# Layer normalisation without affine parameters: separate rings for x and y, tiles of 8 rows, and bn_stats parts combined by GpSimd

## The chip, the cores and the metric

The kernel runs on one core of one Trainium2 chip. The metric is the device time of one execution in microseconds. Each comparison runs both kernels in alternating rounds on the same chip. All runs used here are fast, with the granted clock at 1.0. The profile's span is about 2 us shorter than the time. The changed kernel was timed in one batch and the experiments in three others; the kernel before ran in every batch, and its medians there agree within 0.1 us.

## The reference

```python
def setup_inputs():
    batch, seq, dim = 32, 512, 1024
    return {"x": np.random.randn(batch, seq, dim).astype(np.float32), "eps": 1e-5}

def reference(x, eps):
    mean = np.mean(x, axis=-1, keepdims=True)
    var = np.var(x, axis=-1, keepdims=True)
    return ((x - mean) / np.sqrt(var + eps)).astype(np.float32)
```

There are 16384 rows of 1024 floats: 67.11 MB are read and 67.11 MB are written. With 128 partitions each partition handles 128 rows; "a tile of K rows" below means K rows per partition, and each row is 4 KB there.

## The kernel before

A tile has 4 rows per partition. Loads go out on the SyncE queue and stores on the ScalarE queue; there are six buffers for x and six for y, 48 rows of 4 KB in each partition. A scheduler orders the instructions.

```python
    K = 4
    xin = ctx.enter_context(tc.tile_pool(name="xin", bufs=6))
    yout = ctx.enter_context(tc.tile_pool(name="yout", bufs=6))
    ...
    for t in range(ntiles):                                   # 32 tiles
        xt = xin.tile([P, K, D], fdt)
        nc.sync.dma_start(out=xt, in_=x2[rows].rearrange("(p k) d -> p k d", p=P))
        for k in range(K):
            for s in range(NSUB):                             # two halves of a row
                nc.vector.bn_stats(...)
            nc.vector.bn_aggr(out=mv[:, k, :], in_=stats[:, k, :, :])
        ...                                                   # -mean, var + eps, reciprocal on VectorE
        nc.scalar.activation(out=rstd, in_=ivar, func=AF.Sqrt, bias=0.0, scale=1.0)
        nc.gpsimd.tensor_mul(out=nmr, in0=negmean, in1=rstd)
        for k in range(K):
            nc.scalar.activation(out=yt[:, k, :], in_=xt[:, k, :], func=AF.Identity,
                                 bias=nmr[:, k : k + 1], scale=rstd[:, k : k + 1])
        nc.scalar.dma_start(out=dst, in_=yt)
```

## Time and profile before

| What | Value |
|---|---|
| time | 321.23 us (321.14 to 321.33) |
| span of the profiled run | 319.0 us |
| DMA, mean over the span | 421 GB/s, digit 9 in 38 of 40 slices |
| VectorE / ScalarE / GpSimd busy | 57% / 48% / 2% |

The prediction below shows the lines behind this table and reads them. One more part of the page, the DMA part, has the number of packets (one record for each piece that one DMA engine moves) and, per queue, the packets, the bytes and the time of the packets as a share of 16 engines:

```profile
DMA packets 9222, 134.27 MB, mean 421 GB/s; under 512 B 1024, under 2 KB 1024, under 8 KB 1024
...
q1 hardware_dynamic: 4608, 67.11, 49.6%
q10 hardware_dynamic: 4608, 67.11, 49.2%
```

Each queue has 4096 data packets, 67.11 MB / 4096 = 16 KB, which is the 4 rows of a tile in one partition, and 512 small ones, 16 for each of its 32 transfers. Queue q1 carries the loads and q10 the stores.

### The profile page before, as it was taken

Reading aid. Unit: us, or ns where it says so; the run is one execution under the profiler, and the core shown is the slowest. Engines: PE = TensorE matmul, PEld = TensorE weight load, DVE = VectorE, ACT = ScalarE, POOL = GpSimd, SP = SyncE. Lnnn points to the kernel's source line nnn. Section 1 sums busy time; section 2 is a strip of 40 time slices with the busy share of each in tenths; the row PEclk is TensorE's granted clock in tenths of the full one; section 3 lists DMA queues with packets and bytes.
Section 4 is the critical chain, followed back from the end, with each engine's and each line's share of the span. In section 5 each row is a group of like instructions: output and inputs, shape, how many; then the busy total and the mean of one; then the engine's idle time right before and its main releaser. Section 6 shows DMA issues by size and latency. Waiting matters only on the chain.

```text
span 319.0 us, 926 instructions
## 1 busy us (share of the span) xinstructions
DVE 181.6 (57%) x480; ACT 154.3 (48%) x161; POOL 6.6 (2%) x36
## 2 busy tenths in 40 slices
DVE  0999764457754477544676355765446744467610
ACT  1147491651907419074380833809247091470970
POOL 0000000000000000000000000000000000000000
DMA  7999999999999999999999999999999999999995
GB/s 294 427 405 422 438 431 431 431 429 431 426 429 432 435 431 431 429 427 431 431 433 435 430 431 427 427 431 427 435 438 430 428 431 427 431 427 427 421 427 220
DMA packets 9222, 134.27 MB, mean 421 GB/s; under 512 B 1024, under 2 KB 1024, under 8 KB 1024
## 3 DMA queue, kind: packets, MB, share of 16 engines
q1 hardware_dynamic: 4608, 67.11, 49.6%
q10 hardware_dynamic: 4608, 67.11, 49.2%
q14 instruction: 6, 0.05, 0.0%
HBM read 67.11 MB, written 67.11 MB: 421 GB/s over the span
## 4 chain that ended last, share of the span: by engine, by line
DMA 87%; DVE 4%; issue 3%; ACT 2%; SPq 1%; POOLq 0%; POOL 0%; DVEq 0%
DMA xt<-in_x_dram 87%; DVE stats L53 3%; ACT yt L75 1%; SPq L47 1%; DVE mv L57 0%; DVE ivar L65 0%; DVE negmean L59 0%; POOLq L115 0%; ACT rstd L68 0%; POOL nmr L71 0%; DVE vpe L61 0%; DVEq L65 0%; DVEq L59 0%
## 5 line engine op out<-in xcount | busy, mean ns | idle before, releaser
L53 DVE BATCH_NORM_STATS2 stats<-xt 128x6 f32<-128x512 f32 x256 | 159.4, 665 | 115.3 <-DMA xt<-in_x_dram 115.3
L75 ACT ACTIVATE yt<-xt,nmr,rstd 128x1024 f32<-128x1024 f32 x128 | 146.7, 1227 | 4.7 <-POOL nmr L71 4.5
L68 ACT ACTIVATE rstd<-ivar 128x4 f32<-128x4 f32 x32 | 6.6, 205 | 149.6 <-DVE ivar L65 149.0
L57 DVE BATCH_NORM_AGGREGATE mv<-stats 128x2 f32<-128x12 f32 x128 | 25.1, 196 | 1.1
L71 POOL TENSOR_TENSOR nmr<-negmean,rstd 128x4 f32<-128x4 f32 x32 | 6.3, 198 | 297.9 <-ACT rstd L68 297.9
L65 DVE RECIPROCAL ivar<-vpe 128x4 f32<-128x4 f32 x32 | 5.7, 178 | 3.0
L59 DVE TENSOR_SCALAR negmean<-mv 128x4 f32<-128x4 f32 x32 | 5.4, 170 | 3.1
L61 DVE TENSOR_SCALAR vpe<-mv 128x4 f32<-128x4 f32 x32 | 5.2, 162 | 0.0
L68 ACT ACT_TABLE_LOAD x1 | 1.3, 1283 | 0.7 <-PEq L101 0.7
L101 POOL MEMSET const-float32-0.0<- 128x1 f32 x1 | 0.1, 98 | 0.2 <-issue 0.2
L101 POOL MEMSET const-uint8-127<- 128x1 uint8 x1 | 0.1, 102 | 0.0
L101 POOL MEMSET const-bfloat16-1.0<- 128x1 bf16 x1 | 0.1, 101 | 0.0
L101 POOL MEMSET const-float32-1.0<- 128x1 f32 x1 | 0.1, 98 | 0.0
## 6 DMA issues: line engine op xcount, KB each, us to landing
xt<-in_x_dram SPq DMA_DIRECT2D x32, 2048.0 KB, 38.4
out_dram<-yt ACTq DMA_DIRECT2D x32, 2048.0 KB, 15.5
```

The lines of the kernel that those rows point to most:

```text
L47: nc.sync.dma_start(out=xt, in_=x2[rows].rearrange("(p k) d -> p k d", p=P))
L53: nc.vector.bn_stats(out=stats[:, k, s, :], in_=xt[:, k, s * BN_MAX : (s + 1) * BN_MAX],)
L57: nc.vector.bn_aggr(out=mv[:, k, :], in_=stats[:, k, :, :])
L59: nc.vector.tensor_scalar_mul(out=negmean, in0=mv[:, :, 0], scalar1=-1.0)
L61: nc.vector.tensor_scalar(out=vpe, in0=mv[:, :, 1], scalar1=eps_val, scalar2=None, op0=ALU.add)
L65: nc.vector.reciprocal(out=ivar, in_=vpe)
L68: nc.scalar.activation(out=rstd, in_=ivar, func=AF.Sqrt, bias=0.0, scale=1.0)
L71: nc.gpsimd.tensor_mul(out=nmr, in0=negmean, in1=rstd)
L75: nc.scalar.activation(out=yt[:, k, :], in_=xt[:, k, :], func=AF.Identity, bias=nmr[:, k : k + 1], scale=rstd[:, k : k + 1],)
L101: nc = _bacc.Bacc("TRN2", target_bir_lowering=False, num_devices=1)
```

## The change

The intent is to take the aggregation off VectorE, by combining the parts of bn_stats for eight rows at once on GpSimd, and to use larger tiles: fifteen of 8 rows, then 4, 2, 2. The 48 rows of buffer are kept, divided into a ring of 32 for x and one of 16 for y. The order of instructions is the one written, not a scheduler's.

```diff
+TILES = (8, 8, 8, 8, 8, 8, 8, 8, 8, 8, 8, 8, 8, 8, 8, 4, 2, 2)
+XRING = 32
+YRING = 16
+GROUP = 8
...
-    xin = ctx.enter_context(tc.tile_pool(name="xin", bufs=6))
-    yout = ctx.enter_context(tc.tile_pool(name="yout", bufs=6))
+    xr = rings.tile([P, XRING, D], fdt)
+    yr = rings.tile([P, YRING, D], fdt)
...
-            nc.vector.bn_aggr(out=mv[:, k, :], in_=stats[:, k, :, :])
+        pool_sum(nmean[:, :G], mean4)             # two GpSimd adds
+        nc.gpsimd.tensor_scalar(... scalar1=-1.0 / H, op0=ALU.mult)
+        nc.gpsimd.tensor_tensor(out=dev[:, :G], in0=mean4, in1=<nmean broadcast>, op=ALU.add)
+        nc.gpsimd.tensor_mul(out=dev[:, :G], in0=dev[:, :G], in1=dev[:, :G])
+        nc.gpsimd.tensor_scalar(... scalar1=float(D // H), op0=ALU.mult)
+        nc.gpsimd.tensor_tensor(out=dev[:, :G], in0=dev[:, :G], in1=m2, op=ALU.add)
+        pool_sum(ss[:, :G], dev[:, :G])           # two GpSimd adds
+        nc.scalar.activation(out=std[:, :G], in_=ss[:, :G], func=AF.Sqrt, bias=eps_t, scale=1.0 / D)
+        nc.vector.reciprocal(out=rstd[:, :G], in_=std[:, :G])
...
+    with tc.manual_schedule():
+        for (K, row, xp), (_, _, yp) in zip(place(TILES, XRING), place(TILES, YRING)):
+            nc.sync.dma_start(out=xr[:, xp : xp + K, :], in_=rows_of(x2, row, K))
+            ...
+                group(xr[:, a : a + G, :], yr[:, b : b + G, :], G)
+            nc.scalar.dma_start(out=rows_of(o2, row, K), in_=yr[:, yp : yp + K, :])
```

More of the change, by code (lines that the diff above doesn't have):

```diff
@@ L7, with place @@
 from concourse._compat import with_exitstack
+TILES = (8, 8, 8, 8, 8, 8, 8, 8, 8, 8, 8, 8, 8, 8, 8, 4, 2, 2)
+XRING = 32
+YRING = 16
+GROUP = 8
+def place(tiles, ring):
+    plan, row, pos = [], 0, 0
+    for K in tiles:
+        if pos + K > ring:
+            pos = 0
+        plan.append((K, row, pos))
+        row += K
+        pos += K
+    return plan
 @with_exitstack
@@ L26 @@
     BN_MAX = nc.vector.BN_STATS_FMAX
-    assert D % BN_MAX == 0
     NSUB = D // BN_MAX
-    K = 4
-    rows_per_tile = P * K
-    assert N % rows_per_tile == 0
-    ntiles = N // rows_per_tile
-    xin = ctx.enter_context(tc.tile_pool(name="xin", bufs=6))
-    yout = ctx.enter_context(tc.tile_pool(name="yout", bufs=6))
+    assert sum(TILES) * P == N
+    rings = ctx.enter_context(tc.tile_pool(name="rings", bufs=1))
     st = ctx.enter_context(tc.tile_pool(name="st", bufs=4))
@@ L41, with rows_of, pool_sum, group @@
     ALU = mybir.AluOpType
-    for t in range(ntiles):
-        rows = slice(t * rows_per_tile, (t + 1) * rows_per_tile)
-        xt = xin.tile([P, K, D], fdt)
-        nc.sync.dma_start(out=xt, in_=x2[rows].rearrange("(p k) d -> p k d", p=P))
-        stats = st.tile([P, K, NSUB, 6], fdt)
-        mv = st.tile([P, K, 2], fdt)
-        for k in range(K):
+    xr = rings.tile([P, XRING, D], fdt)
+    yr = rings.tile([P, YRING, D], fdt)
+    eps_t = rings.tile([P, 1], fdt)
+    def rows_of(a, row, K):
+        return a[row * P : (row + K) * P].rearrange("(p k) d -> p k d", p=P)
+    def pool_sum(o, terms):
+        G = terms.shape[1]
+        half = st.tile([P, GROUP, 2], fdt, name="half")
+        nc.gpsimd.tensor_tensor(
+            out=half[:, :G], in0=terms[:, :, 0:2], in1=terms[:, :, 2:4], op=ALU.add
+        )
+        nc.gpsimd.tensor_tensor(
+            out=o, in0=half[:, :G, 0], in1=half[:, :G, 1], op=ALU.add
+        )
+    def group(xs, ys, G):
+        stats = st.tile([P, GROUP, NSUB, 6], fdt, name="stats")
+        for k in range(G):
             for s in range(NSUB):
@@ L54 @@
                     out=stats[:, k, s, :],
-                    in_=xt[:, k, s * BN_MAX : (s + 1) * BN_MAX],
+                    in_=xs[:, k, s * BN_MAX : (s + 1) * BN_MAX],
                 )
-            nc.vector.bn_aggr(out=mv[:, k, :], in_=stats[:, k, :, :])
-        negmean = st.tile([P, K], fdt)
-        nc.vector.tensor_scalar_mul(out=negmean, in0=mv[:, :, 0], scalar1=-1.0)
-        vpe = st.tile([P, K], fdt)
-        nc.vector.tensor_scalar(
-            out=vpe, in0=mv[:, :, 1], scalar1=eps_val, scalar2=None, op0=ALU.add
-        )
@@ L64 @@
-        ivar = st.tile([P, K], fdt)
-        nc.vector.reciprocal(out=ivar, in_=vpe)
-        rstd = st.tile([P, K], fdt)
-        nc.scalar.activation(out=rstd, in_=ivar, func=AF.Sqrt, bias=0.0, scale=1.0)
-        nmr = st.tile([P, K], fdt)
-        nc.gpsimd.tensor_mul(out=nmr, in0=negmean, in1=rstd)
-        yt = yout.tile([P, K, D], fdt)
-        for k in range(K):
+        H = 2 * NSUB
+        parts = stats[:, :G].rearrange("p g s (h c) -> p g (s h) c", h=2)
+        mean4, m2 = parts[:, :, :, 1], parts[:, :, :, 2]
@@ new lines, in group @@
+        nmean = st.tile([P, GROUP], fdt, name="nmean")
+        dev = st.tile([P, GROUP, H], fdt, name="dev")
+        ss = st.tile([P, GROUP], fdt, name="ss")
+        pool_sum(nmean[:, :G], mean4)
+        nc.gpsimd.tensor_scalar(
+            out=nmean[:, :G], in0=nmean[:, :G], scalar1=-1.0 / H, scalar2=None, op0=ALU.mult
+        )
+        nc.gpsimd.tensor_tensor(
+            out=dev[:, :G],
+            in0=mean4,
+            in1=nmean[:, :G].unsqueeze(2).to_broadcast([P, G, H]),
+            op=ALU.add,
+        )
@@ new lines, in group @@
+        nc.gpsimd.tensor_mul(out=dev[:, :G], in0=dev[:, :G], in1=dev[:, :G])
+        nc.gpsimd.tensor_scalar(
+            out=dev[:, :G], in0=dev[:, :G], scalar1=float(D // H), scalar2=None, op0=ALU.mult
+        )
+        nc.gpsimd.tensor_tensor(out=dev[:, :G], in0=dev[:, :G], in1=m2, op=ALU.add)
+        pool_sum(ss[:, :G], dev[:, :G])
+        std = st.tile([P, GROUP], fdt, name="std")
+        nc.scalar.activation(
+            out=std[:, :G], in_=ss[:, :G], func=AF.Sqrt, bias=eps_t, scale=1.0 / D
+        )
@@ L75 @@
+        rstd = st.tile([P, GROUP], fdt, name="rstd")
+        nc.vector.reciprocal(out=rstd[:, :G], in_=std[:, :G])
+        nmr = st.tile([P, GROUP], fdt, name="nmr")
+        nc.gpsimd.tensor_mul(out=nmr[:, :G], in0=nmean[:, :G], in1=rstd[:, :G])
+        for k in range(G):
             nc.scalar.activation(
-                out=yt[:, k, :],
-                in_=xt[:, k, :],
+                out=ys[:, k, :],
+                in_=xs[:, k, :],
                 func=AF.Identity,
@@ L81 @@
             )
-        dst = o2[rows].rearrange("(p k) d -> p k d", p=P)
-        nc.scalar.dma_start(out=dst, in_=yt)
+    with tc.manual_schedule():
+        nc.vector.memset(eps_t, eps_val)
+        for (K, row, xp), (_, _, yp) in zip(place(TILES, XRING), place(TILES, YRING)):
+            nc.sync.dma_start(out=xr[:, xp : xp + K, :], in_=rows_of(x2, row, K))
+            for g in range(0, K, GROUP):
+                G = min(GROUP, K - g)
+                a, b = xp + g, yp + g
+                group(xr[:, a : a + G, :], yr[:, b : b + G, :], G)
+            nc.scalar.dma_start(out=rows_of(o2, row, K), in_=yr[:, yp : yp + K, :])
 _INS = ['x', 'eps']
```

## The prediction

> **What bounds the kernel now.** I read the span slices first, because they say whether one resource is full from end to end.
>
> ```profile
> span 319.0 us, 926 instructions
> ...
> DVE 181.6 (57%) x480; ACT 154.3 (48%) x161; POOL 6.6 (2%) x36
> ...
> DMA  7999999999999999999999999999999999999995
> GB/s 294 427 405 422 438 431 431 431 429 431 426 429 432 435 431 431 429 427 431 431 433 435 430 431 427 427 431 427 435 438 430 428 431 427 431 427 427 421 427 220
> ```
>
> No compute engine is over 57% busy, while the DMA digit is 9 in 38 of 40 slices; only the first and the last slice are not full. Next the chain that ended last and the groups of instructions:
>
> ```profile
> DMA xt<-in_x_dram 87%; DVE stats L53 3%; ACT yt L75 1%; SPq L47 1%; DVE mv L57 0%; DVE ivar L65 0%; DVE negmean L59 0%; POOLq L115 0%; ACT rstd L68 0%; POOL nmr L71 0%; DVE vpe L61 0%; DVEq L65 0%; DVEq L59 0%
> ...
> L53 DVE BATCH_NORM_STATS2 stats<-xt 128x6 f32<-128x512 f32 x256 | 159.4, 665 | 115.3 <-DMA xt<-in_x_dram 115.3
> L75 ACT ACTIVATE yt<-xt,nmr,rstd 128x1024 f32<-128x1024 f32 x128 | 146.7, 1227 | 4.7 <-POOL nmr L71 4.5
> ...
> L57 DVE BATCH_NORM_AGGREGATE mv<-stats 128x2 f32<-128x12 f32 x128 | 25.1, 196 | 1.1
> L71 POOL TENSOR_TENSOR nmr<-negmean,rstd 128x4 f32<-128x4 f32 x32 | 6.3, 198 | 297.9 <-ACT rstd L68 297.9
> ```
>
> VectorE's 115.3 us of idle time before the statistics is all waiting for loads: compute follows the data. Last the stretches (stretch, its length, busy time of DVE, ACT and POOL, clock, DMA share, GB/s):
>
> ```profile
> 0.00:4.00 4.00, 0.00 (x0) 1.28 (x1) 0.20 (x4) 1.00 0.55 143
> 4.00:8.00 4.00, 0.00 (x0) 0.00 (x0) 0.00 (x0) 1.00 1.04 442
> ...
> 20.00:24.00 4.00, 4.00 (x10) 0.21 (x1) 0.20 (x1) 1.00 0.98 373
> ...
> 160.00:200.00 40.00, 22.75 (x60) 19.48 (x21) 0.79 (x4) 1.00 1.01 431
> ...
> 308.00:312.00 4.00, 0.00 (x0) 1.34 (x2) 0.00 (x0) 1.00 0.97 414
> 312.00:316.00 4.00, 0.00 (x0) 0.00 (x0) 0.00 (x0) 1.00 0.80 340
> 316.00:319.00 3.00, 0.00 (x0) 0.00 (x0) 0.00 (x0) 1.00 0.04 16
> ```
>
> The rate is 430 to 432 GB/s in every 40 us stretch from 40 to 280 us, with reads and writes mixed, and much the same with reads alone (442 in 4 to 8 us). The bytes are fixed: 67.11 read and 67.11 written. 134.22 MB / 431 GB/s = 311.4 us. Of the span of 319.0 only 7.6 us are not streaming at 431: the start (4 x (431 - 143) / 431 = 2.7 us), the dip when the first store joins (4 x (431 - 373) / 431 = 0.5 us), the end (312 to 319 us carries 1360 + 48 KB, which is 3.3 us of work, so 3.7 us are lost), and 0.7 us of small dips. A change that leaves the bytes alone can gain from these 7.6 us and nowhere else, unless it raises the 431.
>
> **What the Trainium skill says.** "DMA: Bandwidth & Descriptors", section "Where 436 GB/s comes from", puts the ceiling of a core's DMA ports at 435.2 GB/s. The trace agrees: 431 is 99% of it, so larger transfers can add about 1%, or 3 us, at best. The same passage says that an HBM share of some 358 GB/s binds; the measured 431 contradicts that here, with one core running. "Queues, rings and completion order" of that page says that each DMA engine alternates between its queues packet by packet. The trace agrees: the two queues take 49.6% and 49.2%. "GPSIMD Engine Reference", section 3.1, gives about 2.6 cycles of 1.2 GHz per element for a two-input operation; no instruction of before is long enough to test it (198 ns for 4 elements a partition is nearly all fixed cost).
>
> **The change part by part.** Removed from VectorE: 128 aggregations (25.1 us), and 64 small tensor-scalars (10.6 us); 32 reciprocals become 18. All of that ran beside full DMA, so removing it is worth nothing by itself. Added: per tile nine GpSimd instructions, each waiting for the semaphore of the one before it, as the order of the built program shows. By the row of nmr a 4-element one takes 198 ns; the nine have 8 to 32 elements, at 2.6 cycles / 1.2 GHz = 2.2 ns each beyond four (an estimate from the GPSIMD page): 9 x 198 + 0.32 us = 2.1 us, and with gaps of 0.08 us (in the timeline of before, from the end of rstd to nmr) 2.7 us per tile. The 18 tiles pay about 49 us of GpSimd, in the idle time of an engine that was 2% busy.
>
> The serial chain of one 8-row tile, from the pitches in the timeline of before (0.575 us from one bn_stats to the next, 1.133 us from one row of ACT to the next): 16 bn_stats 15 x 0.575 + 0.67 = 9.3 us, GpSimd 2.7, then Sqrt, reciprocal and nmr at about 0.2 each plus gaps 0.8, ACT 7 x 1.133 + 1.23 = 9.2 us. In the new order VectorE starts tile i+1 only after the reciprocal of tile i, so the statistics cannot repeat faster than 9.3 + 2.7 + 0.8 = 12.8 us. The DMA's own period is 8.39 MB / 431 = 19.5 us, so this is hidden while reads and writes overlap.
>
> The buffers hold 48 rows as before (24 + 24), now 32 for x and 16 for y. **Head.** The first 4.19 MB arrive by 4 + (4194 - 572) / 435 = 12.3 us, with 1.15 us to the wake-up (before: 2097 KB are reached at 7.45, the first bn_stats starts at 8.60), so at 13.45. Statistics end at 22.75, ACT starts at 26.3, the first store is issued at 35.5 us, where before it was at 19.6. But four tiles of loads, 16.8 MB, keep the DMA busy until about 41 us, and load 4 is released at 35.5 as well: no idle DMA. Reads alone and both together run at the same rate, so the late first store only shifts writes to the end. **Middle.** With two y slots, ACT on tile i starts when store i-2 has landed. In 19.5 us it needs 1.2 (landing) + 9.2 + 1.3 (issue to first byte) = 11.7, 7.8 us before the queue would run dry. Loads have about 18 us of slack. **End.** Before the first store flows at 36.6 us, 572 + 435 x 32.6 = 14.8 MB are read. The rest, 52.3 MB at 215.5 GB/s, ends at 279.3 us, and 14.8 MB of writes are left: 0.52 of store 12, stores 13 and 14, and the tiles of 4, 2, 2 rows. Now stores drain at 4.19 MB / 431 = 9.7 us, and a y slot needs 11.7 to come back. Store 12 drains at 284.4; ACT on tile 14 runs 285.7 to 294.9; its bytes flow from 296.1, while store 13 has drained at 294.1: one **gap of 2.0 us**. The small tiles follow without one: tile 15's store is issued at 300.3, 16's about 303.5, 17's about 308.9, and store 14 drains at 305.9, then 310.7, 313.2, 315.6. With the 3.7 us between effective end of bytes and end of span, that is 319.3.
>
> By difference: span 319.0 + 2.0 (gap), less 0.7 for the dips of 401 GB/s around 298 to 306 us and of 310 to 311 us, which the split tail should fill, + 0 for everything that moved on the compute engines = 320.3. The time of before is 2.2 us above its span, so 322.5; the clock sum gives 321.5. I choose 322.0.
>
> **Rivals.**
> (1) The larger transfers raise the rate. For: half as many descriptors of twice the size (32 KB per partition) and fewer transfer boundaries, 36 for 64. Against: 431 of 435 is used already. At 434 GB/s the bytes take 309.3 us, and the time is about 320.
> (2) GpSimd is slower than I take it, and the chain statistics, GpSimd, Sqrt, reciprocal becomes the bound at the end. For: nine dependent steps, a stride of 12 bytes in the reads, nothing of the kind in the profile of before. At 0.6 us each a tile pays 5.4 us: still below 19.5 in the middle, but the last two tiles each wait 2.7 us longer, so the time is some 325.
> (3) Two y slots are too few: a landing that takes several us longer lets the write queue run dry in the middle. Loads then take the free share and finish earlier, and the write-only end grows to as much as five tiles with a 2 us gap each: 329. Against: 7.8 us of slack; stores in before land 8.8 to 20.4 us after their issue, queueing included.
> (4) The freed VectorE makes it faster, as the change intends. Against: VectorE's idle time was 115.3 us and all of it waited for loads. It would make nothing of the time.
>
> **Range and chances.** The floor is start + bytes + end, 2.7 + 309.3 + 3.7 + 2.2 = 317.9 at 434 GB/s; the 2% border is at 314.8, below it, so faster is nearly excluded. Slower needs 327.7, which takes rival 3 or 2 and 3 together. I put 319.3 to 325.5 as the range: rival 1 at its best and rival 2 at its worst are just inside. Chances: faster 0.01, same 0.95, slower 0.04.
>
> **What would show it.** Right: DMA digits of 9 and about 431 GB/s from the second slice to the last but two; VectorE near 9.3 x 16 = 150 us and GpSimd near 50; the first store issued at about 35 us; ACT waiting for stores in the middle; a stretch of lower GB/s near 294 to 296 us. Wrong: middle slices clearly off 431 (rivals 1 and 3), GpSimd steps over 0.4 us, or several dips in the last 40 us.

## The result, and the profile after

The changed kernel took 318.09 us (318.04 to 318.25) against 321.28 us in the same rounds. The ratio is 0.9902, with a 95% interval of 0.9888 to 0.9916. A ratio here is the mean time of one kernel's fast runs over that of the other's of the same rounds, so it is not quite the ratio of the quoted medians. It is 1% faster, inside the 2% that was given a chance of 0.95, but 1.2 us below the stated range of 319.3 to 325.5.

The head of the page of the changed kernel, its DMA part and the first groups of instructions:

```profile
span 316.3 us, 749 instructions
...
DVE 155.6 (49%) x275; ACT 153.4 (49%) x147; POOL 41.5 (13%) x184
...
DMA  8999989999999999999999999999999999999996
...
DMA packets 5189, 134.26 MB, mean 425 GB/s; under 512 B 576, under 2 KB 576, under 8 KB 576
...
q1 hardware_dynamic: 2592, 67.11, 49.7%
q10 hardware_dynamic: 2592, 67.11, 49.2%
...
L113 ACT ACTIVATE yr<-xr,nmr,rstd 128x1024 f32<-128x1024 f32 x128 | 146.7, 1227 | 117.8 <-DMA out_dram<-yr 115.7
L77 DVE BATCH_NORM_STATS2 stats<-xr 128x6 f32<-128x512 f32 x256 | 153.4, 677 | 12.2 <-DMA xr<-in_x_dram 12.2
```

The reader sees that the DMA is still the bound, that VectorE lost 26 us of work and GpSimd gained 35, and that the waiting moved: VectorE hardly waits for loads now, and ScalarE waits 115.7 us for a store to free a y slot. The packets fell from 9222 to 5189, because a tile of 8 rows gives packets of 32 KB.

The stretches of the changed kernel (stretch, its length, busy time of DVE, ACT and POOL, clock, DMA share, GB/s):

```profile
0.00:4.00 4.00, 0.06 (x1) 1.28 (x1) 0.19 (x4) 1.00 0.72 246
4.00:8.00 4.00, 0.00 (x0) 0.00 (x0) 0.00 (x0) 1.00 0.95 410
...
160.00:200.00 40.00, 19.40 (x34) 20.22 (x21) 5.64 (x25) 1.00 1.00 433
...
292.00:296.00 4.00, 2.58 (x5) 0.84 (x3) 0.29 (x2) 1.00 0.95 408
296.00:300.00 4.00, 0.00 (x0) 4.00 (x4) 1.79 (x9) 1.00 1.04 451
...
308.00:312.00 4.00, 0.00 (x0) 1.74 (x2) 0.00 (x0) 1.00 0.97 410
312.00:316.00 4.00, 0.00 (x0) 0.00 (x0) 0.00 (x0) 1.00 0.40 168
```

The span fell by 2.7 us, and the bytes moved per stretch say where. (The view counts a whole packet in the stretch in which it starts. Up to 16 packets of 32 KB, 0.5 MB or 1.2 us of work, are under way at a border, so each of the three terms below can be off by some tenths of a us.) **Middle:** the six stretches from 40 to 280 us have a mean of 432.5 GB/s, where before had 431.0: 240 x 1.5 / 431 = 0.8 us. **Start:** by 280 us the changed kernel has moved 0.69 MB more in all; less the 0.36 MB of the middle, 0.33 MB or some 0.75 us come from the first 40 us. **End:** from 280 us to the end of the span, before moves 14.9 MB in 39.0 us and the changed kernel 14.3 MB in 36.3 us. At 431 GB/s these would take 34.7 and 33.1 us, so 4.3 and 3.2 us are lost: 1.1 us gained. The sum is 2.7 us.

The dip that was forecast near 294 to 296 us is not there: 408 and 451 GB/s. The timeline of ScalarE in the changed kernel shows why the forecast failed. Each of these starts was released by a store that freed a y slot:

```profile
236.35 9.16 ACT L113 ACTIVATE yr<-xr,nmr,rstd 128x1024 f32<-128x1024 f32 x8 [9.41 <-DMA out_dram<-yr]
...
255.74 9.16 ACT L113 ACTIVATE yr<-xr,nmr,rstd 128x1024 f32<-128x1024 f32 x8 [9.49 <-DMA out_dram<-yr]
...
270.83 9.16 ACT L113 ACTIVATE yr<-xr,nmr,rstd 128x1024 f32<-128x1024 f32 x8 [5.21 <-DMA out_dram<-yr]
...
283.35 9.16 ACT L113 ACTIVATE yr<-xr,nmr,rstd 128x1024 f32<-128x1024 f32 x8 [2.65 <-DMA out_dram<-yr]
```

The stores land 19.4 us apart while loads and stores share equally, and then 15.1 and 12.5 us apart, although loads are still in flight. The loads at that time are those of the 4-, 2- and 2-row tiles, with packets of 16 and 8 KB against 32 KB of the stores. If the engines alternate packet by packet, the stores get 32/48 and 32/40 of the rate: 4.19 MB / (433 x 2/3) = 14.5 us and 4.19 / (433 x 4/5) = 12.1 us. That is close to what was measured. The DMA part of the page, asked for one window only, shows the shares directly (packets, MB, share of the engines' time). First 256 to 270 us, mostly 16 KB loads, then 270 to 280 us, mostly 8 KB loads:

```profile
q10 hardware_dynamic: 142, 4.16, 68.9%
q1 hardware_dynamic: 129, 1.87, 31.2%
```

```profile
q10 hardware_dynamic: 109, 3.54, 81.9%
q1 hardware_dynamic: 111, 0.91, 21.5%
```

The stores have 69% and 80% of the bytes, against 2/3 and 4/5. As a consequence the loads last longer: from 280 to 292 us they still move 1.43 MB, where the forecast had the last load end at 279.3 us. The trace does not name a packet's engine, but if each packet is joined to the one that ended within 40 ns of its start, 16 chains come out, and from 273.5 to 281 us 139 of 141 steps in them go from one queue to the other. What this does to the time was the main theory to test (theory S below).

### The profile page after: what moved, and what is told of

Read it like the earlier page. It is cut to its first block, busy times and chain, and to the rows that moved or that the text cites. A ratio compares the mean times of both kernels' runs of the same rounds, so it can differ in the third digit from the quotient of the medians.

```text
span 316.3 us, 749 instructions
## 1 busy us (share of the span) xinstructions
DVE 155.6 (49%) x275; ACT 153.4 (49%) x147; POOL 41.5 (13%) x184
## 2 busy tenths in 40 slices
DMA packets 5189, 134.26 MB, mean 425 GB/s; under 512 B 576, under 2 KB 576, under 8 KB 576
## 3 DMA queue, kind: packets, MB, share of 16 engines
q1 hardware_dynamic: 2592, 67.11, 49.7%
q10 hardware_dynamic: 2592, 67.11, 49.2%
HBM read 67.11 MB, written 67.11 MB: 424 GB/s over the span
## 4 chain that ended last, share of the span: by engine, by line
DMA 65%; ACT 23%; DVE 7%; POOL 2%; issue 1%; ACTq 0%; POOLq 0%
DMA out_dram<-yr 61%; ACT yr L113 23%; DVE stats L77 7%; DMA xr<-in_x_dram 4%; POOL half L66 0%; ACT std L105 0%; POOL dev L99 0%; POOL dev L102 0%; POOL dev L92 0%; POOL nmean L89 0%; POOL dev L98 0%; POOL nmean L69 0%; POOL ss L69 0%; DVE rstd L109 0%; ACTq L129 0%
## 5 line engine op out<-in xcount | busy, mean ns | idle before, releaser
L113 ACT ACTIVATE yr<-xr,nmr,rstd 128x1024 f32<-128x1024 f32 x128 | 146.7, 1227 | 117.8 <-DMA out_dram<-yr 115.7
L77 DVE BATCH_NORM_STATS2 stats<-xr 128x6 f32<-128x512 f32 x256 | 153.4, 677 | 12.2 <-DMA xr<-in_x_dram 12.2
L66 POOL TENSOR_TENSOR half<-stats 128x16 f32<-128x16 f32 (+2 forms) x18 | 4.2, 232 | 161.3 <-DVE stats L77 161.3
L105 ACT ACTIVATE std<-ss,eps_t 128x8 f32<-128x8 f32 (+2 forms) x18 | 5.4, 300 | 37.6 <-POOL ss L69 31.5
L99 POOL TENSOR_SCALAR dev<-dev 128x32 f32<-128x32 f32 (+2 forms) x18 | 5.2, 291 | 1.6
L102 POOL TENSOR_TENSOR dev<-dev,stats 128x32 f32<-128x32 f32 (+2 forms) x18 | 4.5, 251 | 1.5
L92 POOL TENSOR_TENSOR dev<-stats,nmean 128x32 f32<-128x32 f32 (+2 forms) x18 | 4.3, 238 | 1.5
L98 POOL TENSOR_TENSOR dev<-dev 128x32 f32<-128x32 f32 (+2 forms) x18 | 4.2, 234 | 1.4
L89 POOL TENSOR_SCALAR nmean<-nmean 128x8 f32<-128x8 f32 (+2 forms) x18 | 4.2, 231 | 1.6
L66 POOL TENSOR_TENSOR half<-dev 128x16 f32<-128x16 f32 (+2 forms) x18 | 3.9, 214 | 1.4
## 6 DMA issues: line engine op xcount, KB each, us to landing
out_dram<-yr ACTq DMA_DIRECT2D x15, 4096.0 KB, 29.4
```

Of the source, the lines that this page charges most:

```text
L66: nc.gpsimd.tensor_tensor(out=half[:, :G], in0=terms[:, :, 0:2], in1=terms[:, :, 2:4], op=ALU.add)
L77: nc.vector.bn_stats(out=stats[:, k, s, :], in_=xs[:, k, s * BN_MAX : (s + 1) * BN_MAX],)
L89: nc.gpsimd.tensor_scalar(out=nmean[:, :G], in0=nmean[:, :G], scalar1=-1.0 / H, scalar2=None, op0=ALU.mult)
L92: nc.gpsimd.tensor_tensor(out=dev[:, :G], in0=mean4, in1=nmean[:, :G].unsqueeze(2).to_broadcast([P, G, H]), op=ALU.add,)
L98: nc.gpsimd.tensor_mul(out=dev[:, :G], in0=dev[:, :G], in1=dev[:, :G])
L99: nc.gpsimd.tensor_scalar(out=dev[:, :G], in0=dev[:, :G], scalar1=float(D // H), scalar2=None, op0=ALU.mult)
```

## The experiments

Twelve kernels were run, all with correct results. Times are medians; the kernel before took 321.20 to 321.29 us beside them.

### pad16 and pad4: the packet size alone

A gap of 32 bytes after every fourth row (pad16) or every row (pad4) in both rings splits the packets, with the same instructions, tiles, transfers and waits.

```diff
-    xr = rings.tile([P, XRING, D], fdt)
-    yr = rings.tile([P, YRING, D], fdt)
+    xr = rings.tile([P, XRING // PK, PK * D + PAD], fdt)      # pad16: PK = 4; pad4: PK = 1; PAD = 8
+    yr = rings.tile([P, YRING // PK, PK * D + PAD], fdt)
```

> The changed kernel with nothing altered but a gap of 32 bytes after every fourth row of both rings, so that one DMA packet carries 16 KB as before the change and not 32 KB; the same tiles, instructions, transfers and waits. Theory A (fixed cost per packet): by the pages, the change took 4033 packets (9222 to 5189), 252 per DMA engine, and the engines' busy time fell from 98.8% of 319.0 = 315.2 us to 98.9% of 316.3 = 312.8 us, 9.4 ns per packet. Here 240 packets per engine come back: +2.3 us, about 320.4 us. Theory B (the gain is from the short tail and the start alone, the packet size does nothing): 318.1 us. Theory C (GpSimd in place of VectorE): 318.1 us as well.

> The same with a gap after every row: packets of 4 KB. Theory A: 28160 packets more than in the changed kernel, 1760 per DMA engine, at 9.4 ns: +16.5 us, about 334.6 us, in proportion to the count. Theory B and C: 318.1 us.

Measured: pad16 321.63 us, 3.5 us above the changed kernel; pad4 329.05 us, 11 above. So packet size does matter, which theories B and C deny, but the sizes of theory A are wrong in both: too small for pad16, too large for pad4. The stretches tell the two effects apart. First pad16, then pad4:

```profile
200.00:240.00 40.00, 19.39 (x34) 20.08 (x21) 5.17 (x23) 1.00 1.01 432
...
292.00:296.00 4.00, 0.00 (x0) 4.00 (x5) 0.00 (x0) 1.00 0.78 332
296.00:300.00 4.00, 2.35 (x5) 2.85 (x4) 0.20 (x1) 1.00 0.63 266
```

```profile
200.00:240.00 40.00, 18.73 (x34) 18.91 (x18) 4.64 (x20) 1.00 1.02 422
...
300.00:304.00 4.00, 0.00 (x0) 3.81 (x4) 0.00 (x0) 1.00 0.62 252
304.00:308.00 4.00, 2.58 (x5) 3.05 (x4) 0.62 (x4) 1.00 0.76 306
```

In both the forecast dip is back. In pad16 it is worth (408 + 451 - 332 - 266) x 4 / 431 = 2.4 us against the same stretches of the changed kernel. The rest is the rate: the mean from 40 to 280 us is 430.8 against 432.5, worth 0.9 us. A fixed cost per packet fits the three rates. One engine has a sixteenth of the rate, so an engine takes 155 ns for a packet of 4 KB at 422 GB/s, 608 ns for 16 KB at 431 and 1211 ns for 32 KB at 433. From 4 to 16 KB that is 151 ns for each further 4 KB, which leaves an estimated 4 to 5 ns per packet. The 9.4 ns that the expectation took from the busy shares are about twice that: the DMA shares of 1.01 and 1.02 in small-packet runs show records that overlap.

### a_aggr: GpSimd undone

```diff
+        for k in range(G):
+            nc.vector.bn_aggr(out=mv[:, k, :], in_=stats[:, k, :, :])
-        pool_sum(nmean[:, :G], mean4)
-        ...  (the nine GpSimd instructions)
```

> The changed kernel with the GpSimd part undone: eight aggregations and one scaling on VectorE per tile in place of the nine GpSimd instructions; rings, tiles, packets and order held. Theories A and B: 318.1 us within 0.5, since none of this work is on the DMA's path except in the last tiles, where both chains cost about the same (8 x 0.12 against 2.7 us per tile of 8). Theory C: most of the 3.2 us is lost, about 321 us.

Measured: 318.89 us, ratio 0.9927 (0.9915 to 0.9940). Most of the gain stays without any GpSimd combination. The 0.8 us that are missing are more than the expectation allowed. From 40 to 280 us it moves as much (mean 432.5 GB/s), and its last store is issued earlier (307.1 against 309.8 us). What differs is the very end, with 25 and 16 GB/s in 314 to 315 and 315 to 316 us, about the rate of one engine of 16 (27). The changed kernel has 33 there and then 0, and the kernel before ends with 49, 33 and 16 GB/s from 315 to 318 us. That one engine lags is an inference from the rate, and why was not settled.

### a_notail: sixteen tiles of 8 rows

```diff
-TILES = (8, ..., 8, 4, 2, 2)
+TILES = (8,) * 16
```

> The changed kernel with sixteen tiles of 8 rows, no 4, 2, 2 at the end. Theory B (short tail): the last tile's ACT then takes 9.2 us from the landing of store 13 at 296.0, its store is issued at 305.4, flows from 306.4 and needs 9.7 us, where store 14 has drained at about 304.2: +2.5 us or more, about 320.6 us. If the tail split does nothing for the time: 318.1 us.

Measured: 321.02 us, 2.9 above the changed kernel. The size was as expected, but the profile shows the dip (279 and 262 GB/s in 292 to 296 and 296 to 300 us), so the tail split does more than shorten the last tile. The next run separates the two.

### load8: the last eight rows loaded at once

```diff
-            nc.sync.dma_start(out=xr[:, xp : xp + K, :], in_=rows_of(x2, row, K))
+            if row < 120: ...                                  # as before
+            elif row == 120:
+                nc.sync.dma_start(out=xr[:, xp : xp + 8, :], in_=rows_of(x2, row, 8))
```

> The changed kernel, but the last eight rows are loaded by one transfer of 32 KB packets and not by three of 16, 8 and 8 KB; compute and stores keep the split 4, 2, 2. Theory S (share by packet size: the engines alternate packet by packet, so the small packets of the last loads left two thirds and then four fifths of the rate to the stores, and this is why the forecast dip near 294 us did not come): reads and writes share equally to the end, the store landings before ACT's last 8-row tiles stay 19.4 us apart instead of 15.1 and 12.5, a stretch of under 350 GB/s comes back after the reads end, and the time is 318.1 + about 2 = 320 us. Theory B (only the short compute and store tail counts): 318.1 us, no dip.

Measured: 319.87 us, ratio 0.9966. Compute and stores are split 4, 2, 2 as in the changed kernel; the packets of the last loads grew, and 1.8 us are gone. (Two small things moved along: the last stores follow the load's mapping of rows to partitions, with the same packet sizes, and the 4-row group waits for all eight rows.) The timeline of ScalarE and a stretch of load8:

```profile
255.41 9.16 ACT L113 ACTIVATE yr<-xr,nmr,rstd 128x1024 f32<-128x1024 f32 x8 [9.48 <-DMA out_dram<-yr]
...
274.71 9.16 ACT L113 ACTIVATE yr<-xr,nmr,rstd 128x1024 f32<-128x1024 f32 x8 [9.43 <-DMA out_dram<-yr]
```

```profile
292.00:296.00 4.00, 0.00 (x0) 3.58 (x5) 0.20 (x1) 1.00 0.61 262
```

The landings are 19.3 us apart again, where the changed kernel had 15.1, the load queue moves no data after 278 us, and the dip is back. Theory S holds here in time, spacing and dip. The small loads of the tail help mainly because they yield to the stores while they last, and so stretch the time in which both queues have work: the stores then land 12.5 us apart and not the 9.7 us of stores alone, and a y slot, which the forecast gave 11.7 us to come back, is free in time.

### x16 and y16: unequal packets all the way

The padding is put into one ring only: loads of 16 KB against stores of 32 KB (x16), and the mirror (y16).

```diff
-    xr = rings.tile([P, XRING, D], fdt)
+    xr = rings.tile([P, XRING // PK, PK * D + XPAD], fdt)      # x16: XPAD = 8, YPAD = 0; y16: 0 and 8
```

> The changed kernel with a gap after every fourth row of the x ring alone: loads in 16 KB packets, stores in 32 KB. Theory S: stores get two thirds, a store lands some 20 us after its issue and not 29.4, reads and writes stay closer together, no dip at the end; the added packets cost about half of what the middle of pad16 lost (431 against 433 GB/s), 0.6 us: about 318.5 us. Theory A (fixed cost per packet alone, 120 packets more per engine, with everything of pad16's +3.5 us due to it): 319.9 us.

> The mirror: stores in 16 KB packets, loads in 32 KB; the same number of packets as x16. Theory S: loads get two thirds, run as far ahead as the x ring lets them, and the stretch of stores alone at the end grows, with a dip of 2 us or more: 320.7 us or above, at least 1.5 us over x16. Theory A: the same as x16.

Measured: x16 330.0 us, y16 332.54 us. Neither the fixed cost nor theory S's forecast of the time comes close, though the share itself is confirmed (from 270 to 280 us x16 moves 3.01 MB of stores beside 1.31 MB of loads). These are the DMA issues of x16 (count, size, median time from issue to landing):

```profile
xr<-in_x_dram SPq DMA_DIRECT2D x15, 4096.0 KB, 56.7
out_dram<-yr ACTq DMA_DIRECT2D x15, 4096.0 KB, 19.5
```

In x16 a store lands 19.5 us after its issue, as expected (some 20), and 29.4 in the changed kernel. But the stores then catch up with the loads, no finished tiles are left to be stored (VectorE waits 100.1 us for loads, against 12.2 in the changed kernel), and after the last 8-row load the DMA has no work while the statistics and ScalarE run. The stretches of x16:

```profile
296.00:300.00 4.00, 3.50 (x7) 3.28 (x4) 0.33 (x2) 1.00 0.28 119
300.00:304.00 4.00, 1.45 (x3) 4.00 (x5) 1.82 (x9) 1.00 0.04 16
304.00:308.00 4.00, 1.08 (x3) 3.06 (x4) 0.33 (x2) 1.00 0.30 131
```

That is (3 x 431 - 119 - 16 - 131) x 4 / 431 = 9.5 us. In y16 the loads run ahead until the x ring has no free slot, and then the stores run alone (97.8% of the engines' time from 154 to 159 us) until they run dry too, with 274 GB/s from 160 to 164 us: 397 to 405 GB/s in every 40 us stretch from 120 to 280 us. The order of the two and their distance (2.5 us) were right; that they lose 12 and 14 us against the changed kernel was missed. Equal packets in the body, and smaller loads only at the end, is the good case, and the changed kernel has it.

### b_tiles: the tile sizes in the kernel before

```diff
-    K = 4
+    TILES = (8,) * 15 + (4, 2, 2)
-    xin = ctx.enter_context(tc.tile_pool(name="xin", bufs=6))
-    yout = ctx.enter_context(tc.tile_pool(name="yout", bufs=6))
+    xin = ctx.enter_context(tc.tile_pool(name="xin", bufs=3))     # buffers of 8 rows
+    yout = ctx.enter_context(tc.tile_pool(name="yout", bufs=3))
```

> The kernel before with only the tile sizes of the changed one (fifteen tiles of 8 rows, then 4, 2, 2; pools of 3 and 3 buffers of 8 rows): aggregation on VectorE, the scheduler's order, the old instructions. If packets and tails make the gain and not GpSimd or the rings: 318.1 us within 0.7. If the rings 32 and 16 or the new order are needed: 320 us or more.

Measured: 331.57 us, ratio 1.0317: 10 us slower than before. The larger tiles alone lose. Two holes show in the profile. In the stretches the DMA falls to 341 GB/s in 20 to 40 us, and to 152 and 68 GB/s in 284 to 292 us; for the second, the timeline of ScalarE has this:

```profile
267.31 4.62 ACT L76 ACTIVATE yt<-xt,nmr,rstd 128x1024 f32<-128x1024 f32 x4
281.61 0.21 ACT L69 ACTIVATE rstd<-ivar 128x8 f32<-128x8 f32 x1 [9.68 <-DVE ivar L66]
291.09 0.20 ACT L69 ACTIVATE rstd<-ivar 128x4 f32<-128x4 f32 x1 [9.27 <-DVE ivar L66]
291.10 0.34 ACTq L85 DMA_DIRECT2D out_dram<-yt  x1
```

The rows are finished at 271.9 us and their store is issued at 291.1, behind the square roots of later tiles, which wait for loads.

### a_r24 and b_r32: rings and order apart

a_r24 is the changed kernel with XRING = 24 and YRING = 24; b_r32 is b_tiles with four x and two y buffers.

> The changed kernel with rings of 24 and 24 rows in place of 32 and 16. Theory R (8-row tiles need four x slots): three loads are 12.6 MB and are used up at about 31 us, while ACT frees the first slot at 35.5: the hole that the tile sizes alone showed in the kernel before (341 GB/s in 20 to 40 us, some 4 us) comes back, 322 us or above. Theory O (the order of instructions alone matters, with every store issued right behind its own tile's ACT): no hole, 318 to 319 us.

> The kernel before with the tile sizes of the changed one and pools of four x and two y buffers (32 and 16 rows), in the scheduler's order. Theory R: this mends the loss of the tile sizes alone, 318 to 319 us. Theory O: the scheduler puts a tile's store behind the next tile's square root, which waits for the next load (store issued at 291.1 us, its rows done at 271.9, in that run); with two y buffers this hurts more, 325 us or above.

Measured: a_r24 326.21 us, b_r32 325.59 us (324.1 to 328.4). Both theories hold, each for its own loss. With 24 x rows the hole at the start is there in the written order too; this stretch of a_r24 loses (419 - 288) x 20 / 431 = 6 us against the changed kernel, which has a mean of 419 there:

```profile
20.00:40.00 20.00, 13.56 (x26) 10.61 (x11) 4.63 (x20) 1.00 0.73 288
```

With 32 x rows that hole is closed in the old code (417 GB/s in b_r32), but its ends still have gaps: 332 and 346 GB/s in 280 to 288 us, 270 and 262 in 304 to 312 us. a_aggr, with the same rings, tiles and aggregation on VectorE but in the written order, took 318.89 us, so some 6.7 us go with the order, as near as b_r32's wide spread allows. One thing is not separated from it: the pools of b_r32 give each small tail tile a whole buffer of 8 rows, the rings do not. In these runs 8-row tiles need both the unequal rings and the written order.

### a_t4: the changed kernel with 4-row tiles

```diff
-TILES = (8, ..., 8, 4, 2, 2)
+TILES = (4,) * 32
```

> The changed kernel with thirty-two tiles of 4 rows: rings, GpSimd part and order kept, packets of 16 KB, equal packets for loads and stores to the end. If the gain lies in packets and tail and not in GpSimd, rings or order: like the kernel before, 320.5 to 321.5 us. If GpSimd, rings or order gain by themselves: 318 to 319 us.

Measured: 320.58 us, ratio 0.9976 (0.9963 to 0.9990). It lies nearly where before is, at 429 to 433 GB/s in the middle. Rings, order and GpSimd together give 0.6 us here without the larger tiles. A stretch of 184 GB/s in 308 to 312 us costs it (431 - 184) x 4 / 431 = 2.3 us at the end, so without that it might have been better; this was not tried.

### a_tail1: an attempt to beat both

```diff
-TILES = (8, ..., 8, 4, 2, 2)
+TILES = (8,) * 15 + (4, 2, 1, 1)
```

> An attempt to beat both: the last two rows as two tiles of one. If the end is set by the chain of the last tile (statistics, GpSimd, ACT), the last store's 0.5 MB flows 1.2 us sooner: 317 us. If the DMA queue is still full when the last store is issued (about 410 GB/s from 304 to 313 us in the changed kernel says so): 318.1 us within 0.4.

Measured: 318.21 us, ratio 0.9907: no gain. The DMA still moves 400 GB/s in 308 to 312 us, when the last store is issued, so a shorter last chain is worth nothing. No version that beats the changed kernel was found.

## Why the prediction was right or wrong

**The bound.** Right. The DMA was the bound before and is after, and the aggregation that left VectorE was worth little: a_aggr, with it back on VectorE, keeps 2.4 of the 3.2 us.

**The head.** Right within 0.4 us: first bn_stats at 13.10 (forecast 13.45), ACT at 26.44 (26.3), first store issued at 35.63 (35.5), no idle DMA before it. One term was wrong without harm: the first store's bytes were to flow 1.3 us after its issue, but from 35 to 40 us the load queue alone moves data, and the store begins only after 40 us.

**GpSimd.** Right in kind: from 22.77 to 25.55 us the nine instructions of the first tile take 2.8 us (forecast 2.7). In sum they are busy 41.5 us and not 49, as the gaps were counted into the 49. Rival 2 did not come.

**The middle.** The y slots held, as forecast: no 40 us stretch from 40 to 280 us is below 430 GB/s. The rate was not right. Rival 1, the larger packets, came in part: 432.5 and not 431.0 GB/s, worth 0.8 us, where the estimate had nothing. pad16 and pad4 show that it is the packets. Its "best" of 434 GB/s would have been 2 us, so the rival was named with the right mechanism and about twice the size.

**The end.** This is the step that failed, the overlap of the last loads with the stores: "The rest, 52.3 MB at 215.5 GB/s, ends at 279.3 us" and the "gap of 2.0 us" built on it. In these runs the share was equal only where the packets had equal size. The forecast had quoted that the engines alternate packet by packet, and did not ask how large the packets of the last loads are. They are 16 and 8 KB against 32 KB of the stores; the stores got 69% and 80% of the bytes, store landings came 15.1 and 12.5 us apart, loads ran until about 292 us and not 279.3, and the gap did not open. load8 removes this and brings back a dip of 262 GB/s and 1.8 us; pad16 and pad4 bring it back too. Where loads and stores have equal packets to the end of the loads, the worked-out share and gap are about right: the loads end at 278 us in load8, and its dip, reckoned as for pad16 above, is (408 + 451 - 262 - 393) x 4 / 431 = 1.9 us. (In pad16, with 2.4 us, the last two loads are 8 KB beside stores of 16 KB, so it is equal only in part.) The check that the forecast gave for alternation, "the two queues take 49.6% and 49.2%", could not have failed: both queues of the kernel before move 67.11 MB in packets of 16 KB, whatever the order.

**The last microseconds.** The difference took the end of bytes to end of span as unchanged. From 280 us on it lost 1.1 us less than before, where the estimate had 2.0 - 0.7 = 1.3 us more. The missing gap is 2.0 of these 2.4 us.

**The sum.** Forecast by difference: span 320.3. Measured 316.3, and the terms are 2.4 us at the end, 0.8 in the middle and some 0.75 at the start. The start is the weakest term: first loads of 32 KB packets reach 246 GB/s in the first 4 us and those of 16 KB 143 (131 in pad16), but a packet counts in a stretch by its record. The wake-up of VectorE differs less, 13.10 us in the changed kernel and 13.31 in pad16. By 40 us pad16 has moved 15.98 MB, the changed kernel 16.25 and before 15.90, so with the changed kernel's instructions and smaller packets most of the gain, some 0.6 us, is gone; at the error of these counts that points to packet size without proving it. A further 0.4 us of the miss in the time, not in the span, is that the time was taken as span + 2.2 us and was span + 1.7 (318.04 and 316.3).

**The range.** Its floor had been worked out as 317.9 us in the prediction itself. The low end was put above it, at 319.3: even rival 1's best case of 320 us keeps the gap of 2.0 us.

## What to carry to other kernels

Where two DMA queues shared the engines in these runs, the ratio of their packet sizes was about the ratio of their rates while both had work. A packet's size followed from the contiguous bytes per partition, so a tail split or a padding changes the balance of loads and stores; a balance that was off over the whole kernel cost 12 to 14 us here. In this kernel, whose DMA was full from the start, larger tiles gave 1%, and only with rings that cover the longer first tile and each store issued right behind its own tile.

## What the Trainium skill lacked or had wrong

- "DMA: Bandwidth & Descriptors", section "Queues, rings and completion order": it says that an engine alternates between queues at packet granularity, but not that the share of a queue then follows its packet size. (That the page's packets are the profile's packets of up to 32 KB is not shown.) Here stores of 32 KB beside loads of 16 KB landed 15.1 us apart and not 19.4 (load8: 19.3), and in x16 a store of 4 MB landed 19.5 us after its issue and not 29.4.
- The same page has no rate for large packets of loads and stores together: 422 GB/s with 4 KB packets, 431 with 16 KB, 433 with 32 KB here.
- The same page, section "Where 436 GB/s comes from", says that the HBM side of about 358 GB/s binds for transfers between HBM and SBUF. One core alone reached 433 GB/s here; the page "HBM Reference", section "Specifications (TRN2)", has it right that a core alone goes well above its share.
- "GPSIMD Engine Reference", section 3.1, gives about 2.6 cycles per element for two inputs. Here, from 8 to 32 elements a partition, the squaring grew from 201 to 240 ns, the addition of the mean from 204 to 245 and the addition of m2 from 206 to 259: 1.6, 1.7 and 2.2 ns per element, or 1.95, 2.05 and 2.65 cycles at the 1.2 GHz of that page. So its figure is met by one of the three and is above the other two.
